# A two-layer diffusion trunk on one core: low parts of the weights by an accumulating DMA

## Chip, core and metric

The kernel runs on one core of a Trainium2 chip. The metric is the device time of one execution in microseconds. An engine keeps its own queue and works it in order; the queues wait for each other through semaphores. In the profile PE is TensorE (PEld its weight loads), DVE is VectorE, ACT is ScalarE, POOL is GpSimd, and SP is SyncE, which issues the DMAs of the kernel before.

## What is computed

Two layers over 256 latent tokens and 256 context tokens of width 1024 (the context is dropped after the second layer's mixer). Each layer is a half-step SwiGLU, a mixer (retention in layer 0, neighbourhood attention in layer 1) and another half-step SwiGLU, each behind an RMS norm with scale, shift and gate from a conditioning vector.

```python
def swiglu(x, w_in, w_out):
    a, b = jnp.split(x @ w_in, 2, axis=-1)
    return (jax.nn.silu(a) * b) @ w_out

for i in range(DEPTH):
    ml = (s_c @ w_mod[i] + b_mod[i]).reshape(-1, 3, 3, D)
    h = gated_residual(h, ml, 0, swiglu(ada_in(h, norm_g[i, 0], ml, 0), ffn_w_in[i, 0], ffn_w_out[i, 0]), 0.5)
    ...
    h = gated_residual(h, ml, 1, yl, 1.0)
    ...
    h = gated_residual(h, ml, 2, swiglu(ada_in(h, norm_g[i, 2], ml, 2), ffn_w_in[i, 1], ffn_w_out[i, 1]), 0.5)
return rms_norm(h, final_norm_g)
```

The hidden width is 2816; all inputs are float32.

## The kernel before

**Products in three parts.** The large products run in TensorE's float32r format. Each operand is split in a high part, rounded to that format, and a low part, the rest. A product is then three matmuls: high by high, high by low, low by high (`acc3`, line 623). So every weight tile gives two tiles, `whi` and `wlo`.

**The stream of weights.** `plan_all` lists 200 tiles in the order of use: 88 of `ffn_w_in` (1 MiB each, a tile is 128 partitions by 2048), 64 of `ffn_w_out` (128 by 1408, 704 KB), 32 of retention and 16 of neighbourhood attention (1 MiB each). `load` (272) takes the next one into one of two `raw` buffers by a DMA on SyncE's queue. `prep` (280) takes one of three `whi` and three `wlo` buffers and writes down, for each half of the tile, two steps: `first`, a copy on ScalarE from `raw` to `whi`, and `second`, a subtraction `raw - whi` to `wlo` on the engine in `state["low"]`. That is VectorE but for the first tile or two, whose first halves GpSimd makes (lines 1426 to 1454). `RAWS, SPLITS = 2, 3` (214) are the numbers of buffers. A tile's buffers come free when TensorE has used it up (`retire`, 333); `pump` (303) then splits and loads ahead.

**The order.** All engines but SyncE take their instructions in the order in which the program issues them. A small model of the engines' times (`account`, 131) sets that order while the program is built: after each matmul (`mm`, 261) `advance` (231) issues what is due, such as steps of `soon` (splits of weights), of `later` (normalisation, gating) and of the background. The background (`bg_steps`, 357) makes the conditioning's scale, shift and gate vectors on VectorE from 128 loads of 512 KB (`mraw`, `mod_load`, 348), a step every 2.2 us of the model; `mod_sum` (384) adds each result up in a `one` bank of PSUM while `state["sums"]` is set.

**Stages.** Feed-forward of layer 0, retention with four heads, feed-forward, feed-forward of layer 1, neighbourhood attention with 16 heads, and the last feed-forward, which serves the latent tokens alone. A feed-forward (`ffn`, 734) has two halves of 11 `win` tiles and 8 `wout` tiles. A `win` tile takes 48 matmuls, a `wout` tile 33; they are 512 columns wide for both streams, 258 or 256 in the last one. In each half the first two `wout` tiles run together: both products over ten of eleven parts, then the last part of each, and only then do the two tiles retire. In neighbourhood attention `weigh` (1233) subtracts a mask and a bias on GpSimd for each of 32 units before VectorE reads the scores.

Everything an engine computes through the wrapper `Engine` has line 151, a matmul line 262, a load of `dma` line 166.

Of the kernel before, what the change touches and what calls it, by code (L numbers as in the profile page):

```python
# [9 lines left out]
F32 = mybir.dt.float32  # L10
F32R = mybir.dt.float32r
I32 = mybir.dt.int32
AF = mybir.ActivationFunctionType
ALU = mybir.AluOpType
# [3 lines left out]
P = 128  # L18
# [53 lines left out]
def trunk(ctx, tc, a):  # L72
    nc = tc.nc
# [11 lines left out]
    def nm(s):  # L85
        uid[0] += 1
        return f"{s}_{uid[0]}"
# [8 lines left out]
    def slots2(shape, dt=F32R):  # L96
        return slot(shape, dt), slot(shape, dt)
# [17 lines left out]
    def pair():  # L115
        return ps_pair.tile([P, 2, 512], F32, tag="pair", name=nm("pair"))

    def one():
        return ps_one.tile([P, 512], F32, tag="one", name=nm("one"))
# [4 lines left out]
    now = {"pe": 0.0, "dve": 0.0, "act": 0.0, "pool": 0.0, "dma": 0.0}  # L124
    ready = {}
    HOP = 0.2

    def key(ap):
        return ap.tensor.name

    def account(e, reads, writes, us):
        start = now[e]
        for ap in reads:
            t, by = ready.get(key(ap), (0.0, e))
            start = max(start, t + (HOP if by != e else 0.0))
        now[e] = start + us
        for ap in writes:
            ready[key(ap)] = (now[e], e)
# [23 lines left out]
    A_ = Engine("act", nc.scalar, 0.09, 1200.0)  # L162
# [52 lines left out]
    raws, split_tiles = [], []  # L215
    state = {"loaded": 0, "freed": 0, "split": 0, "retired": 0, "bg_at": 0.0, "hold": True, "sums": True, "inside": True, "lag": (0.0, 0.0), "tight": False}
# [5 lines left out]
    soon = []  # L222
# [49 lines left out]
    def load():  # L272
        src = plan[state["loaded"]]
        state["loaded"] += 1
        w = src.shape[1] * src.shape[2]
        t = wpool.tile([P, 2048], F32, tag="raw", name=nm("raw"), bufs=RAWS)
        dma(out=t[:, :w], in_=src.rearrange("p x y -> p (x y)"))
        raws.append((t, src.shape))

    def prep():  # L280
        raw, shape = raws.pop(0)
        tile_no = state["split"]
        state["split"] += 1
        w = shape[1] * shape[2]
        hi = wpool.tile([P, 2048], F32R, tag="whi", name=nm("whi"), bufs=SPLITS)
        lo = wpool.tile([P, 2048], F32R, tag="wlo", name=nm("wlo"), bufs=SPLITS)
        m = w // 2
        for i, c in enumerate((slice(0, m), slice(m, w))):
            def first(c=c):
                A_.copy(out=hi[:, c], in_=raw[:, c])  # L290

            def second(c=c, i=i):
                state["low"].tensor_tensor(out=lo[:, c], in0=raw[:, c], in1=hi[:, c].bitcast(F32), op=ALU.subtract)
                if i == 1:
                    state["freed"] += 1
                    pump()

            soon.append((now["pe"] + state["lag"][0] + 0.3 + i, tile_no, first, 0, i, raw))
            soon.append((now["pe"] + state["lag"][1] + 1.5 + 1.2 * i, tile_no, second, 1, i, hi))
        soon.sort(key=lambda x: (x[1], x[3], x[4]))  # L300
        split_tiles.append((hi, lo, shape, tile_no))

# [30 lines left out]
    def retire(lag=(0.0, 0.0)):  # L333

        state["retired"] += 1
        state["lag"] = lag
        pump()
        state["lag"] = (0.0, 0.0)
# [125 lines left out]
    sums = {}  # L464
# [441 lines left out]
    def retention(xt, g, done, tab, m, lg):  # L906
# [37 lines left out]
        def proj_v(first):  # L944
            v = [slots2([P, 2, 512]) for _ in range(2)]
            if first:
                ps = [one() for _ in range(4)]
            else:
                pp = [pair(), pair()]
                ps = [pp[t // 2][:, t % 2, :] for t in range(4)]  # L950
            for kh in range(2):
                wh, wl = weight()
                for t in range(4):
                    o = ps[t]
                    for k in range(4):
                        xh = xt[2 * kh + k // 2][0][:, k % 2, t * P:(t + 1) * P]
                        xl = xt[2 * kh + k // 2][1][:, k % 2, t * P:(t + 1) * P]
                        mm(o, lhsT=xh, rhs=wh[:, k, :], start=kh == 0 and k == 0, stop=False)
                        mm(o, lhsT=xh, rhs=wl[:, k, :], start=False, stop=False)
                        mm(o, lhsT=xl, rhs=wh[:, k, :], start=False, stop=kh == 1 and k == 3)  # L960
                    if kh == 1 and first:
                        split(v[t // 2][0][:, t % 2, :], v[t // 2][1][:, t % 2, :], o)
                    elif kh == 1 and t % 2 == 1:
                        split(*v[t // 2], pp[t // 2])
                retire()
            return v

        def scores(q, k, m):
# [108 lines left out]
        for hd in range(H_RET):  # L1077
# [14 lines left out]
            if hd + 1 < H_RET:  # L1092
                m = masks(hd + 1, lg)
# [304 lines left out]
    rows, diag, scale = {}, {}, {}  # L1398
# [88 lines left out]
    for l in range(2):  # L1487
# [8 lines left out]
        else:  # L1496
            raw = neighbourhood(xt, GateLater(lambda: gate(1, 1, (L,), 1.0)), *mixer)
# [10 lines left out]
    y = rstd_rows(L)  # L1508
    for i in range(2):
        for t in range(2):  # L1510
            o, src = slot([P, 512]), out_ps[t][:, i, :]
# [65 lines left out]
```

## Time and profile before

| | us |
|---|---|
| median of 3 runs | 1953.93 (1952.76 to 1954.39) |
| the profiled execution's own time | 1954.45 |
| its span, from the first to the last instruction | 1952.6 |
| TensorE busy | 1923.6 (99%) |
| VectorE busy | 1355.9 (69%) |
| ScalarE busy | 687.2 (35%) |
| GpSimd busy | 89.5 (5%) |

The span is what the trace covers; 1.85 us of the execution lie outside it. Busy time leaves out waiting, branching and the issuing of DMAs. An engine that is busy for 99% of the span sets the time unless its work can be made shorter; the others matter where it waits for them. Matmuls overlap in the records, so the rate of TensorE is read from the number of matmuls in a stretch, not from the mean duration of one.

### The profile page before, as it was taken

What the parts mean: (1) busy time and instruction counts of PE and PEld (TensorE: products, weight loads), DVE (VectorE), ACT (ScalarE), POOL (GpSimd) and SP (SyncE); (2) the same over time, 40 slices, a digit from 0 to 9 for tenths busy, and PEclk for the clock granted to TensorE, in tenths of its full rate; (3) what the DMA queues carried; (4) which work ended last, traced back from release to release, by engine and by line L of the source; (5) the groups of instructions that cost most, each with busy time, mean ns of one, the idle gap of its engine ahead of it and who ended that gap; (6) DMA issues with size and microseconds to landing.
All of it is one profiled execution on the core that took longest, in us unless ns stands there. A gap on an engine that the chain in (4) does not pass through costs nothing.

```text
span 1952.6 us, 26160 instructions
## 1 busy us (share of the span) xinstructions
PE 1923.6 (99%) x10458; PEld 1661.6 (85%) x10458; DVE 1355.9 (69%) x2396; ACT 687.2 (35%) x1033; POOL 89.5 (5%) x116
## 2 busy tenths in 40 slices
PE   7999999999999999999999999999999999999998
PEld 3888888898888888898888889888888899989998
DVE  5676666678888888877667676767632588887665
ACT  4432232333323232342222223322222366665443
POOL 5000000010000000100000001000000101100000
PEclk7999999999999999999999999999999999999999
DMA  7333533434343433234353443555423345544553
GB/s 287 138 136 116 203 130 131 161 119 152 126 144 133 159 130 132 95 130 138 126 189 129 139 138 102 187 194 201 162 101 81 110 119 112 98 116 166 193 174 116
DMA packets 70090, 278.85 MB, mean 143 GB/s; under 512 B 23632, under 2 KB 23888, under 8 KB 52304
## 3 DMA queue, kind: packets, MB, share of 16 engines
q1 hardware_dynamic: 69968, 277.18, 43.3%
q8 instruction: 82, 1.34, 0.3%
q14 instruction: 40, 0.33, 0.1%
HBM read 276.11 MB, written 1.05 MB: 142 GB/s over the span
## 4 chain that ended last, share of the span: by engine, by line
PE 93%; DVE 3%; ACT 2%; DMA 1%; issue 1%; SPq 0%; DVEq 0%; ACTq 0%
PE pair L262 60%; PE one L262 32%; DVE slot L151 1%; DVE t L151 1%; PE one L268 1%; ACT slot L151 1%; ACT whi L151 1%; DVE wlo L151 1%; DVE few L151 0%; DMA h<-in_x 0%; ACT t L151 0%; DMA raw<-in_nv 0%; SPq L166 0%; DVE h L151 0%; DVE scl L151 0%
## 5 line engine op out<-in xcount | busy, mean ns | idle before, releaser
L262 PE MATMUL pair<-slot,whi 128*128 128x512 f32 (+2 forms) x4000 | 1037.8, 351 | 8.2 <-ACT slot L151 5.4
L262 PEld LDWEIGHTS pair<-slot,whi 128*128 128x128 f32 x4000 | 696.3, 190 | 105.6 <-ACT slot L151 6.0
L262 PE MATMUL pair<-slot,wlo 128*128 128x512 f32 (+2 forms) x2000 | 681.0, 349 | 0.0
L262 PE MATMUL one<-slot,whi 128*128 128x512 f32 (+1 forms) x1860 | 481.5, 347 | 0.0
L151 DVE TENSOR_TENSOR wlo<-raw,whi 128x1024 fp32r<-128x1024 f32 (+1 forms) x398 | 433.7, 1121 | 33.6 <-ACT whi L151 32.8
L151 ACT CAST whi<-raw 128x1024 fp32r<-128x1024 f32 (+1 forms) x400 | 365.0, 960 | 224.5 <-PE one L262 140.4
L262 PEld LDWEIGHTS pair<-slot,wlo 128*128 128x128 f32 x2000 | 371.7, 190 | 48.0
L262 PEld LDWEIGHTS one<-slot,whi 128*128 128x128 f32 x1860 | 325.9, 189 | 43.5
L262 PE MATMUL one<-slot,wlo 128*128 128x512 f32 (+1 forms) x930 | 323.1, 347 | 0.0
L151 DVE SCALAR_TENSOR_TENSOR acc<-mraw,sT,acc 128x512 f32<-128x512 f32 x392 | 278.9, 749 | 16.8 <-DMA mraw<-in_wmod 15.5
L151 ACT ACTIVATE t<-pair 128x512 f32<-128x512 f32 x66 | 39.5, 598 | 440.7 <-PE pair L262 440.7
L262 PEld LDWEIGHTS one<-slot,wlo 128*128 128x128 f32 x930 | 176.1, 189 | 21.6
L151 DVE TENSOR_TENSOR t<-pair,t 128x512 f32<-128x512 f32 x66 | 45.6, 691 | 201.8 <-ACT t L151 201.7
L151 DVE TENSOR_TENSOR slot<-t,slot 128x512 fp32r<-128x512 f32 (+2 forms) x144 | 88.2, 613 | 64.9 <-ACT slot L151 63.4
L151 DVE SCALAR_TENSOR_TENSOR h<-one,gate,h 128x256 f32<-128x256 f32 x112 | 49.6, 479 | 106.9 <-PE one L262 106.7
L151 ACT CAST slot<-t 128x512 fp32r<-128x512 f32 (+2 forms) x144 | 79.4, 551 | 123.0 <-DVE t L151 122.7
L151 POOL TENSOR_TENSOR t<-t,t 128x256 f32<-128x256 f32 (+1 forms) x48 | 40.6, 856 | 1687.3 <-ACT t L151 1265.8
L262 PE MATMUL pair<-whi,slot 128*128 128x512 f32 (+1 forms) x384 | 98.5, 339 | 0.0
L262 PE MATMUL one<-slot,slot 128*128 128x512 f32 (+1 forms) x432 | 89.8, 347 | 1.3 <-DVE slot L151 1.0
L151 ACT ACTIVATE t<-h 128x256 f32<-128x256 f32 (+1 forms) x86 | 35.8, 429 | 145.0 <-DVE h L151 129.9
L262 PEld LDWEIGHTS one<-slot,slot 128*128 128x128 f32 x432 | 69.9, 189 | 10.8 <-DVE slot L151 1.4
L262 PEld LDWEIGHTS pair<-whi,slot 128*128 128x128 f32 x384 | 67.1, 189 | 7.5
(103 smaller groups left out, 1103.3 us busy)
## 6 DMA issues: line engine op xcount, KB each, us to landing
raw<-in_win SPq DMA_DIRECT2D x88, 1024.0 KB, 4.9
mraw<-in_wmod SPq DMA_DIRECT2D x128, 512.0 KB, 4.6
raw<-in_wout SPq DMA_DIRECT2D x64, 704.0 KB, 4.1
slot<-in_wmod SPq DMA_DIRECT2D x16, 512.0 KB, 9.7
raw<-in_rv SPq DMA_DIRECT2D x8, 1024.0 KB, 4.8
raw<-in_rg SPq DMA_DIRECT2D x8, 1024.0 KB, 4.8
raw<-in_ro SPq DMA_DIRECT2D x8, 1024.0 KB, 4.9
slot<-in_ex SPq DMA_DIRECT2D x8, 512.0 KB, 5.5
```

The source lines that it names most:

```text
L151: getattr(self.real, op)(*args, **kw)
L262: nc.tensor.matmul(out, lhsT=lhsT, rhs=rhs, start=start, stop=stop)
L268: nc.tensor.transpose(out=out, in_=in_, identity=ident)
```

## The change

`second` no longer subtracts. ScalarE writes the negative of the high part to `wlo`, and a DMA on GpSimd's queue reads the same half tile of the weights from HBM once more and adds it to what stands there: `-whi + raw`. The model counts that DMA, half a tile each, and sets the low part as ready 3 us after it. `second` is due by the first lag, 0.9 us after `first`, instead of the second one. `raws` keeps the source's address for it. `raw` is read by ScalarE's copy alone. In the first head of retention `proj_v` holds `mod_sum` off while it uses its four `one` banks. The choice in `state["low"]` no longer matters.

```diff
-        raws.append((t, src.shape))
+        raws.append((t, src.shape, src))
 
     def prep():
-        raw, shape = raws.pop(0)
+        raw, shape, src = raws.pop(0)
...
             def second(c=c, i=i):
-                state["low"].tensor_tensor(out=lo[:, c], in0=raw[:, c], in1=hi[:, c].bitcast(F32), op=ALU.subtract)
+                A_.activation(out=lo[:, c], in_=hi[:, c].bitcast(F32), func=AF.Copy, scale=-1.0)
+
+                nc.gpsimd.dma_start(out=lo[:, c], in_=src.rearrange("p x y -> p (x y)")[:, c].bitcast(F32R), accum_op=ALU.add)
+                now["dma"] = max(now["dma"], now["act"])
+                account("dma", [], [lo], P * m * 4 / 340e3)
+                ready[key(lo)] = (now["dma"] + 3.0, "dma")
                 if i == 1:
                     state["freed"] += 1
                     pump()
 
             soon.append((now["pe"] + state["lag"][0] + 0.3 + i, tile_no, first, 0, i, raw))
-            soon.append((now["pe"] + state["lag"][1] + 1.5 + 1.2 * i, tile_no, second, 1, i, hi))
+            soon.append((now["pe"] + state["lag"][0] + 1.2 + i, tile_no, second, 1, i, hi))
...
             if first:
+
+                state["sums"] = False
                 ps = [one() for _ in range(4)]
...
+            state["sums"] = True
             return v
```

The order of the instructions at three places follows; a name's number is the tile's own, and x2 stands for two halves in a row.

ScalarE at the start, before (`whi_258` and `whi_260` are the first two weight tiles, `slot_262` and `slot_264` the first normalised chunks that TensorE multiplies):

```order
L151 CAST whi_258<-raw_113 128x1024
L151 ACTIVATE slot_262<-t_62_274,modT 128x256
L151 ACTIVATE slot_262<-t_63_277,modT 128x256
L151 ACTIVATE slot_264<-t_64_281,modT 128x256
L151 CAST whi_260<-raw_115 128x1024
L151 ACTIVATE slot_264<-t_65_287,modT 128x256
```

The same place of the change:

```order
L151 CAST whi_258<-raw_113 128x1024
L151 ACTIVATE wlo_259<-whi_258 128x1024
L151 ACTIVATE slot_262<-t_62_275,modT 128x256
L151 ACTIVATE slot_262<-t_63_278,modT 128x256
L151 ACTIVATE slot_264<-t_64_282,modT 128x256
L151 CAST whi_260<-raw_115 128x1024
L151 ACTIVATE wlo_261<-whi_260 128x1024
L151 ACTIVATE slot_264<-t_65_289,modT 128x256
```

One negation stands ahead of the first chunk and one ahead of the fourth.

ScalarE in the `win` tiles of the last feed-forward, before (`t` is the SiLU of a tile's product, `slot` the high part of the gated product):

```order
L151 CAST whi_15808<-raw_15741 128x1024 x2
L151 ACTIVATE t_2213_15879<-t_2212_15878,few_15881 128x256
L151 CAST slot_15877<-t_2214_15880 128x256
L151 CAST whi_15875<-raw_15832 128x1024 x2
L151 ACTIVATE t_2222_15947<-t_2221_15946,few_15949 128x256
L151 CAST slot_15945<-t_2223_15948 128x256
```

And of the change:

```order
L151 CAST whi_15977<-raw_15895 128x1024 x2
L151 ACTIVATE wlo_15978<-whi_15977 128x1024 x2
L151 ACTIVATE t_2187_16051<-t_2186_16050,few_16053 128x256
L151 CAST slot_16049<-t_2188_16052 128x256
L151 CAST whi_16047<-raw_15965 128x1024 x2
L151 ACTIVATE wlo_16048<-whi_16047 128x1024 x2
L151 ACTIVATE t_2196_16121<-t_2195_16120,few_16123 128x256
L151 CAST slot_16119<-t_2197_16122 128x256
```

Two negations come between the casts of a tile and the next SiLU.

GpSimd in neighbourhood attention, before (each row is the mask's subtraction for one or two units; `t` is the bias that a DMA brought):

```order
L151 TENSOR_TENSOR slot_11650<-slot_11650,t_1751_12745 128x256 x2
L151 TENSOR_TENSOR slot_11650<-slot_11650,t_1767_12861 128x256 x2
L151 TENSOR_TENSOR slot_11650<-slot_11650,t_1786_12985 128x256 x2
L151 TENSOR_TENSOR slot_11650<-slot_11650,t_1809_13092 128x256 x2
L151 TENSOR_TENSOR slot_11650<-slot_11650,t_1830_13195 128x256 x2
```

And of the change:

```order
L151 TENSOR_TENSOR slot_11932<-slot_11932,t_1751_13051 128x256 x2
L295 DMA wlo_13208<-in_nv 128x1024 x2
L151 TENSOR_TENSOR slot_11932<-slot_11932,t_1767_13169 128x256 x2
L295 DMA wlo_13327<-in_nq 128x1024 x2
L151 TENSOR_TENSOR slot_11932<-slot_11932,t_1786_13295 128x256 x2
L151 TENSOR_TENSOR slot_11932<-slot_11932,t_1810_13414 128x256
L295 DMA wlo_13474<-in_nk 128x1024 x2
L151 TENSOR_TENSOR slot_11932<-slot_11932,t_1810_13414 128x256
```

The accumulating DMAs stand between the subtractions in the same queue, two to a weight tile.

## Rows read from the trace of the kernel before

**Rows 1.** The page: its span and its first part, busy time by engine.
```profile
span 1952.6 us, 26160 instructions
PE 1923.6 (99%) x10458; PEld 1661.6 (85%) x10458; DVE 1355.9 (69%) x2396; ACT 687.2 (35%) x1033; POOL 89.5 (5%) x116
```
**Rows 2.** The page: the chain that ended last, by engine.
```profile
PE 93%; DVE 3%; ACT 2%; DMA 1%; issue 1%; SPq 0%; DVEq 0%; ACTq 0%
```
**Rows 3.** Waits of TensorE: who for whom, us in total, times, longest us.
```profile
PEld one L262 <- issue: 15.8, 26, 5.0
PEld pair L262 <- ACT slot L151: 6.0, 3, 3.5
PEld one L262 <- DVE t L151: 4.0, 3, 2.3
...
PEld pair L262 <- DVE t L151: 0.4, 2, 0.2
```
**Rows 4.** Windows: stretch, length, busy us (instructions) by engine, granted clock, DMA share, GB/s.
```profile
15.00:45.00 30.00, 22.33 (x99) 16.01 (x97) 24.50 (x39) 12.99 (x18) 21.71 (x19) 0.72 0.78 313
...
500.00:600.00 100.00, 100.00 (x459) 83.24 (x458) 82.98 (x147) 29.21 (x37) 0.00 (x0) 1.00 0.41 143
...
1300.00:1400.00 100.00, 100.00 (x447) 82.85 (x446) 68.78 (x116) 21.52 (x28) 0.00 (x0) 1.00 0.59 200
...
1800.00:1900.00 100.00, 100.00 (x832) 100.00 (x832) 64.27 (x98) 45.19 (x65) 0.00 (x0) 1.00 0.55 184
```
**Rows 5.** Groups by form, VectorE: busy us, mean ns, idle before, releaser.
```profile
L151 DVE TENSOR_TENSOR wlo<-raw,whi 128x1024 fp32r<-128x1024 f32 x270 | 321.7, 1221 | 19.2 <-ACT whi L151 18.7
...
L151 DVE TENSOR_TENSOR wlo<-raw,whi 128x704 fp32r<-128x704 f32 x128 | 112.0, 910 | 14.4 <-ACT whi L151 14.1
```
**Rows 6.** Groups by form, ScalarE.
```profile
L151 ACT CAST whi<-raw 128x704 fp32r<-128x704 f32 x128 | 93.0, 778 | 106.8 <-PE one L262 38.2 <-DMA raw<-in_wout 34.4 <-issue 32.7
...
L151 ACT ACTIVATE slot<-pair 128x1024 f32<-128x1024 f32 x4 | 4.1, 1029 | 24.3 <-PE pair L262 24.3
```
**Rows 7.** DMA queues (packets, MB, share) and issues (count, KB, us to landing).
```profile
q1 hardware_dynamic: 69968, 277.18, 43.3%
...
raw<-in_wout SPq DMA_DIRECT2D x64, 704.0 KB, 4.1
...
out_y<-slot SPq DMA_DIRECT2D x4, 256.0 KB, 2.4
```
**Rows 8.** DMA from 1800 to 1890 us: rate in 40 slices of 2.25 us.
```profile
GB/s 98 109 215 13 303 16 230 330 80 210 110 198 213 238 23 353 335 113 306 153 302 142 244 226 178 295 36 324 106 106 411 262 160 0 69 382 15 58 368 47
```
**Rows 9.** Timeline of SyncE's queue, last feed-forward: start, us, instruction.
```profile
1720.92 75.89 SPq L166 DMA_DIRECT2D raw<-in_win  x11
1802.55 30.03 SPq L166 DMA_DIRECT2D raw<-in_wout  x8
```
**Rows 10.** The tile raw: durations of one issue on SyncE (min/median/max ns).
```profile
L166 SPq DMA_DIRECT2D raw<-in_win x88: 327/328/430, 11.1 to 1889.6; - x88
```
**Rows 11.** Groups by form, GpSimd.
```profile
L151 POOL TENSOR_TENSOR slot<-slot,t 128x256 f32<-128x256 f32 x32 | 25.0, 782 | 144.9 <-DVE few L151 116.8 <-DMA t<-in_rpb 25.1 <-DVE slot L151 3.0
...
L151 POOL TENSOR_TENSOR wlo<-raw,whi 128x1024 fp32r<-128x1024 f32 x2 | 4.7, 2350 | 3.9 <-ACT whi L151 3.9
```
**Rows 12.** Timeline of TensorE at the start: start, us, instruction, idle before.
```profile
29.65 3.45 PE L262 MATMUL pair<-slot,whi 128*128 128x256 f32 x13 [3.39 <-ACT slot L151]
...
35.57 1.91 PE L262 MATMUL pair<-slot,wlo 128*128 128x256 f32 x8
```
**Rows 13.** Waits of SyncE's queue.
```profile
SPq L166 <- DVE wlo L151: 1327.8, 198, 28.0
```

## Prediction

> **What bounds the kernel now.** I read the page's busy line first: TensorE is busy 1923.6 of 1952.6 us, 99% of the span, so only 29 us can be won without taking matmuls away, and this change takes none away [rows 1]. The chain that ended last says the same: 93% of it is TensorE, 3% VectorE, 1% DMA [rows 2]. TensorE's own waits come next: its longest are start-up and hand-over waits of a few us each, and no row shows it waiting for `wlo` or `whi`; the splits are always ready in time [rows 3]. Then the stages: at 500 to 600 us 16 DMA engines are 41% busy, at 1300 to 1400 us 59%, and at 1800 to 1900 us 55% at 184 GB/s [rows 4]. That last stretch is the last feed-forward (22 `win` tiles, 16 `wout` tiles, latent tokens alone): 832 matmuls in 100 us, 0.120 us each, against 447 and 459, about 0.22 us each, in the full-width stretches of the same rows. There a weight tile is used up in half the time, and DMA has the least room.
>
> **What the change removes.** VectorE loses 398 subtractions, 321.7 + 112.0 = 434 us of its 1355.9 [rows 1, 5]. None of it is on the chain; VectorE is 69% busy and TensorE's waits on it (12 rows, under 4.1 us each, the largest in [rows 3]) come at hand-overs, where small dependent steps follow each other. I book 3 us of gain for shorter queues there.
>
> **What it adds on ScalarE.** 400 negations of half a tile. ScalarE's 128x1024 activation takes 1.03 us, its 704-wide cast 0.78 [rows 6]: 272 x 1.03 + 128 x 0.78 = 380 us on top of 687.2, 55% in all. In the last feed-forward it is 45% busy; two more ops of 1.03 us per 5.77 us (48 matmuls x 0.120) make 81%. It stays off the path, but every small copy that TensorE waits for may now stand behind a negation. I book 3 us, which cancels the gain above.
>
> **What it adds on DMA.** 400 accumulating transfers, a second reading of all weights: 88 x 1024 + 64 x 704 + 48 x 1024 KB = 180 MiB. The trace has no such transfer. What 16 engines need for a plain MiB, called u, has two rows: 43.3% of the span for 277.18 MB is 845 us for 264.3 MiB, 3.20 us [rows 7]; the best slice of the last feed-forward, 411 GB/s, gives 2.55 us [rows 8]. I take the middle, 2.87 us, since packets that wait for each other count as busy in the first and the second is a burst. An accumulate per MiB is at least one load (1 u). It is at most a load, a read of SBUF and a write, each priced like a whole transfer (3 u). I take 2 u: two streams are read, one from HBM like `raw`, one from SBUF like `out_y`, and one is written [rows 7]. With the first load a MiB of weights then costs 3 u = 8.6 us instead of 2.87. No run here prices an accumulate; the Trainium skill (Collectives: The Full Stack, Part 3, on the bandwidth ceiling) has a reducing transfer at half a copy's rate because both sources go through one read ring, and the sum by that price is the same as mine.
>
> *Last feed-forward.* It holds 22 x 1 + 16 x 0.6875 = 33 MiB and 22 x 48 + 16 x 33 = 1584 matmuls, 190.4 us at 0.120. Its loads go out from 1720.9 us on [rows 9]. Three tiles can be split ahead (SPLITS = 3), so 30 MiB must pass while it runs: 30 x 8.61 = 258 us. **258 - 190 = 68 us longer.** This is the main term.
>
> *Full-width stages.* A `win` tile has 48 x 0.224 = 10.8 us. It needs 8.6 us, and the background loads of modulation weights about half a MiB, 1.4 us: 10.0 us, hidden, but only just. Where those loads are densest, 1300 to 1400 us, 200 GB/s is 19.1 MiB, and 9.2 MiB of weights twice more: 37.5 MiB x 2.87 = 108 us in 100 [rows 4]. **8 us.**
>
> *Latency.* With three buffers a tile's low part has two tiles' time to appear, 21.6 us in `win`, which hides everything. Shortest is the place where two `wout` tiles run together and both retire at the end: one tile's time, 33 x 0.224 = 7.4 us. The chain there is two casts and a negation, 3 x 0.78 = 2.3 us [rows 6]; the issue on GpSimd, between SyncE's 0.33 us per DMA [rows 10] and the 2.35 us that GpSimd needs for a subtraction [rows 11], say 1.3; half a `wout` tile at 2 u, 2.0 us; and what landing takes beyond the bytes, 4.1 - 0.69 x 2.87 = 2.1 us [rows 7]. That is 7.7 us alone and some 8.8 beside another load: 1.4 us late at six such places. **8 us.** (The two in the last feed-forward are in its own term.)
>
> *Start.* GpSimd makes the first two low parts in 2.35 us each [rows 11]. TensorE waits 3.39 us for ScalarE's first normalised chunk at 29.65 us and takes the first `wlo` at 35.57 us [rows 12]; one negation now stands before that chunk, one more before its fourth. The accumulate leaves at about 28 us and needs 1.3 + 2.9 + 2.1 = 6.3 us, more beside a queue that is 78% busy from 15 to 45 us [rows 4]. Bounds 0 to 8 us; I take **4 us**.
>
> GpSimd's queue: each accumulate waits in order for its negation, and in neighbourhood attention 32 mask subtractions of 0.78 us stand behind such waits, with VectorE's score pass waiting for them [rows 11]. A negation is at most a few us late and two units of work lie between; I book nothing, and if that cover is gone it is about 1 us at each of 16 tiles. SyncE's queue gains: it waited 1327.8 us in all for VectorE's `wlo` before it could reload `raw`; now the cast alone frees it [rows 13]. That brings loads forward by up to two ScalarE ops and wins nothing, as no row of TensorE waits for them.
>
> **Sum.** 68 + 8 + 8 + 4 = 88 us on the profiled execution's own 1954.45 us (1.85 us of it outside the span), 2042.5; that execution is 0.5 us above the median, so **2042 us**.
>
> **The rivals.** *Hidden.* If the second queue's transfers cost 1 u, the last feed-forward needs 2 x 2.87 = 5.74 us per MiB against 190.4 / 33 = 5.77, and only half the latency and the start remain: about 1960 us, from 1950 to 1995. For it: no stage is above 59% busy now, so a second plain load would fit everywhere on average. Against: two streams must be read for one written. The trace has one data queue [rows 7] and cannot tell whether another has engines of its own; if it had, 2 u = 5.74 us would run beside 2.87 and the result be the same 1960. The Trainium skill (DMA: Bandwidth & Descriptors, "Issuing engines are not separate DMA queues") denies that: all queues share the 16 engines. No run here shows it yet; by it this half of the rival falls and the 88 us stand.
>
> *Dear.* At 3 u the last feed-forward needs 30 x 11.5 - 190 = 154 us more and all transfers together (264.3 + 3 x 180) x 2.87 = 2308 us, so DMA bounds the whole kernel: up to 2330 us; with u = 2.55 the same is 30 x 10.2 - 190 = 116 us and some 2090. Issue on GpSimd leads there too: 76 issues in 190 us leave 2.5 us each, and at 4 us each they cost 304 - 190 = 114 us. For it: GpSimd takes 2.35 us where VectorE takes 1.22 for the same subtraction [rows 5, 11], so slow issue is possible. A mechanism that would stretch the issue is VectorE holding GpSimd off SBUF while it works, 1356 - 434 = 922 us in all; an op of it is 922 us / (2396 - 398) = 0.46 us [rows 1, 5], and if each issue waited for one it would be 1.3 + 0.5 = 1.8 us, still under 2.5, so this alone gives 2042 and not more. The Trainium skill (SBUF — State Buffer, the box on the "DVE blocks DMA" trap) states such a lock for descriptors that GpSimd writes; no row shows it here.
>
> *Faster.* VectorE's relief outweighs the rest. TensorE's waits on VectorE sum to about 20 us over its rows, the largest 4.0 [rows 3]; half of them gone and accumulates free is 1954 - 8 = 1946 us. It decides if an accumulate costs 1 u or less and its landing under 7.4 us. Against it: those waits follow chains of small ops, not the subtractions.
>
> **How the numbers follow.** Forecast case (2000 to 2110 us) 0.48; hidden 0.22, of which 0.05 within 0.2%; dear 0.24; faster 0.06. A measurement of this kernel tells 0.2%, 3.9 us, from no change. So faster 0.06, same 0.05, slower 0.89. The range goes from 1958, above the faster and the unchanged cases (0.11 left out), to 2230, which leaves out the upper part of the dear case (0.09).
>
> **What would show it.** Right: DMA busy share at 0.9 and more in the last feed-forward and TensorE idle there, waiting for DMA into `wlo`, with some 68 us; nearly none in the full-width `win` stages; an accumulate of 512 KB that lands in 5 to 9 us. Wrong: a last feed-forward as long as before (hidden), waits for `wlo` in every stage (dear), GpSimd's issues back to back with idle DMA engines (issue bound), or waits of TensorE that name ScalarE.

## The result and the profile after

The changed kernel takes 2150.03 us (median of 4 runs, 2149.3 to 2150.5) against 1953.95 beside it: 1.100 times the time before, 95% interval 1.099 to 1.102. The forecast was 2042. The sign was right; the loss is 196 us where 88 were worked out.

The page of the kernel after, its span, busy times, DMA queues, chain, GpSimd's issues (busy us, mean ns) and landings (us), against [rows 1], [rows 2] and [rows 7]:

```profile
span 2147.5 us, 26873 instructions
PE 1987.4 (93%) x10458; PEld 1701.2 (79%) x10458; DVE 938.5 (44%) x1998; ACT 1032.7 (48%) x1433; POOL 428.7 (20%) x514
...
q0 software_dynamic: 57600, 188.77, 47.4%
q1 hardware_dynamic: 69968, 277.18, 38.3%
...
PE 70%; DMA 17%; ACT 6%; DVE 3%; issue 2%; POOL 1%; SPq 0%; ACTq 0%; DVEq 0%; POOLq 0%
...
L295 POOL DMA_DIRECT2D wlo<-in_win x176 | 153.2, 874 | 744.4 <-ACT wlo L151 733.2
...
L295 POOL DMA_DIRECT2D wlo<-in_wout x128 | 113.1, 981 | 360.0 <-ACT wlo L151 342.5
...
raw<-in_wout SPq DMA_DIRECT2D x64, 704.0 KB, 6.0
wlo<-in_wout POOLq DMA_DIRECT2D x128, 352.0 KB, 9.2
```

The 195 us of span split in two on the first two rows. TensorE's idle time went from 29.0 to 2147.5 - 1987.4 = 160.1 us, **131 more**. Its busy time grew by 1987.4 - 1923.6 = **64 us** for the same 10458 matmuls, so those took longer. The chain names DMA for 17% of the span, where it was 1%.

What TensorE waits for (who for whom, us in total, times, longest us), against [rows 3]:

```profile
PE pair L262 <- DMA wlo<-in_win: 67.0, 30, 7.4
PE one L262 <- DMA wlo<-in_wout: 35.6, 22, 4.6
PE one L262 <- DMA wlo<-in_rv: 9.5, 2, 8.3
PE pair L262 <- DMA wlo<-in_nk: 7.8, 3, 4.8
...
PE one L262 <- DVE slot L151: 4.4, 3, 2.0
```

Every large row is an accumulate into `wlo` that has not landed. Windows of the same trace, in the columns of [rows 4]:

```profile
15.00:45.00 30.00, 23.05 (x95) 16.12 (x96) 17.99 (x43) 16.54 (x23) 18.45 (x22) 0.66 0.96 350
...
100.00:200.00 100.00, 99.54 (x441) 82.06 (x440) 45.74 (x86) 41.60 (x55) 16.24 (x19) 1.00 0.89 227
500.00:600.00 100.00, 99.76 (x457) 82.71 (x456) 67.01 (x139) 48.06 (x56) 13.88 (x16) 1.00 0.84 229
1300.00:1400.00 100.00, 91.09 (x385) 74.36 (x384) 34.35 (x62) 38.67 (x48) 15.12 (x18) 0.93 0.92 250
...
1900.00:2000.00 100.00, 80.42 (x611) 78.03 (x610) 17.60 (x42) 57.03 (x78) 26.20 (x30) 0.95 1.03 254
```

Inside the full-width stages (100 to 200 us in the first feed-forward, 500 to 600 in retention) TensorE is busy for 99.5% and more, with DMA at 0.89 and 0.84: the accumulates are hidden there. From 1300 to 1400 us its 8.9 us of idle time are two waits of 4.5 and 4.4. In the last feed-forward (here 1867 to 2138 us) DMA is at 1.03 and the matmuls fall from 832 to 611 in 100 us. That stage as a whole, from its first matmul to its last, in the kernel before and after:

```profile
1748.80:1942.90 194.10, 193.41 (x1606) 193.04 (x1606) 127.02 (x209) 86.11 (x134) 5.86 (x7) 1.00 0.47 158
...
1867.40:2137.80 270.40, 216.30 (x1606) 208.46 (x1606) 54.67 (x137) 146.54 (x206) 68.19 (x79) 0.93 0.96 236
```

So where are the other losses? I took the time from the first matmul on a stage's first weight tile to that of the next stage (in the last one, to its last matmul), and subtracted the same time of the kernel before (us longer; FF is a feed-forward; "before last" sums the stages ahead of the last feed-forward). Counted from 0, the stages begin with the weight tiles 0, 38, 70, 108, 146 and 162. The column "us" is the median time, the others are from the profiled execution:

| kernel | us | FF 1 | retention | FF 2 | FF 3 | attention | before last | last FF |
|---|---|---|---|---|---|---|---|---|
| after | 2150.0 | 18.4 | 24.0 | 24.2 | 27.9 | 24.6 | 119 | 76 |
| e1_plain | 2056.4 | 6.9 | 14.3 | 15.8 | 17.2 | 16.6 | 71 | 32 |
| e2_neg_add | 2020.3 | 2.1 | 9.2 | 0.2 | 3.4 | 15.3 | 30 | 37 |
| e3_full_only | 2068.2 | 16.5 | 26.6 | 23.7 | 25.9 | 21.3 | 114 | 0 |
| e4_last_only | 2034.9 | 0.0 | 0.0 | 0.0 | 0.0 | 2.8 | 3 | 74 |
| e5_low_last | 2132.6 | 11.4 | 30.3 | 12.8 | 12.9 | 22.4 | 90 | 90 |
| e6_half | 2043.4 | 12.8 | 18.9 | 8.6 | 12.3 | 6.8 | 59 | 32 |
| e7_neg_first | 2153.0 | 18.9 | 23.3 | 19.1 | 29.0 | 31.0 | 121 | 77 |
| e9_early | 2161.7 | 20.5 | 29.1 | 29.6 | 31.1 | 23.1 | 133 | 76 |
| e10_thin | 2122.8 | 18.7 | 20.8 | 17.8 | 16.7 | 22.3 | 96 | 76 |
| e11_early_thin | 2128.8 | 18.0 | 23.5 | 19.7 | 18.4 | 24.0 | 104 | 73 |
| e12_no_gate | 2117.1 | 17.8 | 15.2 | 13.3 | 14.6 | 24.7 | 86 | 75 |
| e13_no_gate_thin | 2111.3 | 16.3 | 19.4 | 15.7 | 9.9 | 19.9 | 81 | 74 |
| e14_no_gate_low_full | 2016.0 | 9.9 | 10.0 | 12.1 | 8.4 | 21.6 | 62 | 1 |
| e15_raw_behind | 2133.0 | 13.5 | 17.1 | 18.0 | 17.5 | 31.3 | 98 | 81 |
| e16_raw_behind_no_gate | 2114.6 | 12.4 | 13.3 | 16.9 | 9.0 | 22.3 | 74 | 83 |

The last feed-forward lost 76 us, close to the 68 forecast. The stages ahead of it lost 119 where 20 had been booked (8 for full width, 8 for latency, 4 for the start). They lose most of it where one stage hands over to the next: of TensorE's 77 us of waits for low parts there, 43 stand at eight tiles right behind the start of a stage (39, 41, 71, 73, 109, 111, 147 and 148), 16 at the six places where two `wout` tiles run together, 7 at the start and 12 at other tiles. One such place in full: the feed-forward after retention, whose first two `win` tiles run together. The low part of the second, tile 71, lands too late. ScalarE, SyncE, GpSimd and TensorE there (start, us, instruction, idle before):

```profile
874.10 0.51 ACT L151 ACTIVATE slot<-t,modT 128x256 fp32r<-128x256 f32 x1 [0.88 <-DVE t L151]
874.88 0.51 ACT L151 ACTIVATE slot<-t,modT 128x256 fp32r<-128x256 f32 x1 [0.28 <-DVE t L151]
875.30 1.98 ACT L151 CAST whi<-raw 128x1024 fp32r<-128x1024 f32 x2
877.18 2.00 ACT L151 ACTIVATE wlo<-whi 128x1024 fp32r<-128x1024 f32 x2
...
877.30 0.33 SPq L166 DMA_DIRECT2D raw<-in_win  x1
...
878.54 1.81 POOL L295 DMA_DIRECT2D wlo<-in_win  x2 [6.52 <-ACT wlo L151]
...
886.18 2.07 PE L262 MATMUL pair<-slot,wlo 128*128 128x256 f32 x8 [4.59 <-DMA wlo<-in_win]
```

The buffer came free at about 865, with the last matmul on the tile that held it. ScalarE takes the two casts at 875.30, behind the normalisation's chunks; the negations follow, the accumulate of the first half leaves at 878.54, and its sum is there when TensorE goes on at 886.18: 21 us after the buffer was freed, 4.6 of them waited for. At the eight tiles the casts begin 4 to 10 us after the buffer is free, the first accumulate leaves 3 to 4 us later and lands 7 to 12 us after that, 17 to 25 us in all. In the kernel before, the first use of the low part came 12 to 16 us after the buffer was free. The DMA engines between 862 and 900 us, in 40 slices of 0.95 us (busy tenths, GB/s):

```profile
DMA  0000000000000000099999999989699699999200
GB/s 9 0 17 0 0 0 0 0 0 0 0 0 0 0 0 0 0 147 379 414 267 185 112 134 185 211 177 168 233 440 341 78 121 177 203 207 203 52 0 0
```

They are idle for 15 us and then full. The reload of `raw`, freed by the same casts, goes first at about 400 GB/s; the accumulates follow at 110 to 210. After the wait the clock is low (two windows):

```profile
884.60:891.40 6.80, 4.85 (x21) 4.56 (x22) 1.16 (x3) 4.23 (x6) 1.73 (x2) 0.50 0.99 246
...
895.30:902.10 6.80, 6.80 (x59) 6.80 (x58) 0.29 (x1) 0.60 (x1) 0.00 (x0) 1.00 0.33 66
```

At a granted clock of 0.50, 1.2 GHz, 21 matmuls take 4.85 us, 0.23 us each; at 1.00 (2.4 GHz) 59 take 6.80, 0.115. The trace has 22 such stretches, 159 us in all, against 4 before, 28 us; one goes with each of TensorE's 17 longest waits for a low part. TensorE is busy for 113 us of them, before for 18; at half the clock that makes (113 - 18) / 2 = 48 of the 64 us of busy time. The other 16 I did not trace. The mean granted clock fell from 0.993 to 0.963.

### The profile page after: what moved, and what is told of

The parts are those of the page before. It is cut to its first block, busy times and chain, and to the rows that moved or that the text cites. A ratio compares the mean times of both kernels' runs of the same rounds, so it can differ in the third digit from the quotient of the medians.

```text
span 2147.5 us, 26873 instructions
## 1 busy us (share of the span) xinstructions
PE 1987.4 (93%) x10458; PEld 1701.2 (79%) x10458; DVE 938.5 (44%) x1998; ACT 1032.7 (48%) x1433; POOL 428.7 (20%) x514
## 3 DMA queue, kind: packets, MB, share of 16 engines
q0 software_dynamic: 57600, 188.77, 47.4%
q1 hardware_dynamic: 69968, 277.18, 38.3%
## 4 chain that ended last, share of the span: by engine, by line
PE 70%; DMA 17%; ACT 6%; DVE 3%; issue 2%; POOL 1%; SPq 0%; ACTq 0%; DVEq 0%; POOLq 0%
PE pair L262 46%; PE one L262 23%; DMA wlo<-in_win 7%; DMA wlo<-in_wout 5%; ACT whi L151 2%; DMA wlo<-in_ro 2%; DVE t L151 2%; ACT wlo L151 2%; DVE slot L151 1%; ACT t L151 1%; POOL wlo L295 1%; ACT slot L151 1%; PE one L268 1%; DMA wlo<-in_nv 1%; DMA wlo<-in_rv 1%
## 5 line engine op out<-in xcount | busy, mean ns | idle before, releaser
L262 PE MATMUL pair<-slot,whi 128*128 128x512 f32 (+2 forms) x4000 | 1054.7, 355 | 4.2 <-ACT slot L151 3.0
L262 PEld LDWEIGHTS pair<-slot,whi 128*128 128x128 f32 x4000 | 710.8, 194 | 102.8 <-ACT slot L151 3.9
L262 PE MATMUL pair<-slot,wlo 128*128 128x512 f32 (+2 forms) x2000 | 702.3, 361 | 79.3 <-DMA wlo<-in_win 67.0
L262 PEld LDWEIGHTS pair<-slot,wlo 128*128 128x128 f32 x2000 | 385.9, 198 | 137.2 <-DMA wlo<-in_win 74.7
L262 PE MATMUL one<-slot,whi 128*128 128x512 f32 (+1 forms) x1860 | 489.1, 352 | 0.0
L151 ACT ACTIVATE wlo<-whi 128x1024 fp32r<-128x1024 f32 (+1 forms) x400 | 366.8, 965 | 0.3
L262 PEld LDWEIGHTS one<-slot,whi 128*128 128x128 f32 x1860 | 331.8, 193 | 44.2
L262 PE MATMUL one<-slot,wlo 128*128 128x512 f32 (+1 forms) x930 | 330.6, 355 | 38.3 <-DMA wlo<-in_wout 35.6
L295 POOL DMA_DIRECT2D wlo<-in_win x176 | 153.2, 874 | 744.4 <-ACT wlo L151 733.2
L295 POOL DMA_DIRECT2D wlo<-in_wout x128 | 113.1, 981 | 360.0 <-ACT wlo L151 342.5
## 6 DMA issues: line engine op xcount, KB each, us to landing
wlo<-in_win POOLq DMA_DIRECT2D x176, 512.0 KB, 10.3
```

The costliest lines, as they stand in the source:

```text
L151: getattr(self.real, op)(*args, **kw)
L262: nc.tensor.matmul(out, lhsT=lhsT, rhs=rhs, start=start, stop=stop)
L295: nc.gpsimd.dma_start(out=lo[:, c], in_=src.rearrange("p x y -> p (x y)")[:, c].bitcast(F32R), accum_op=ALU.add)
```

## The experiments

In the diffs a minus is the kernel after, but for e8.

**e3 and e4: which stages.** The accumulate where the condition holds, VectorE's subtraction with its old due time elsewhere (e4: `tile_no >= 160`). The last feed-forward has 38 tiles, 162 to 199, and not the 40 of the two expectations: tiles 160 and 161 are the last two of attention. Where expectations speak of 121 and 75 us, the table has 119 and 76.

```diff
-                A_.activation(out=lo[:, c], in_=hi[:, c].bitcast(F32), func=AF.Copy, scale=-1.0)
+                if tile_no < 160:
+                    A_.activation(out=lo[:, c], in_=hi[:, c].bitcast(F32), func=AF.Copy, scale=-1.0)
...
+                else:
+                    state["low"].tensor_tensor(out=lo[:, c], in0=raw[:, c], in1=hi[:, c].bitcast(F32), op=ALU.subtract)
```

> Accumulates for weight tiles 0 to 159, the subtraction on VectorE as before for the last feed-forward's 40 tiles. Theory that the stages' losses add: the last feed-forward's 75 us go, 2150 - 75 = 2075 us, within 10. If the loss in the full-width stages were only what was forecast (20 us): 1975 us.

> The subtraction on VectorE as before for weight tiles 0 to 159, accumulates for the last feed-forward's 40 tiles. Theory that the last feed-forward is bound by the DMA engines at 3 copies' time per MiB: 1954 + 75 = 2029 us, within 10. If its loss came from work left over from the crowded stages before it: under 2000 us.

Measured 2068.2 and 2034.9 us, both as expected. Their losses, 114 and 80 us, add up to the whole; the 3 us of e4 in attention are those two tiles. e4's last feed-forward is full as in the changed kernel (window 1830 to 1930):

```profile
1830.00:1930.00 100.00, 78.96 (x567) 75.47 (x567) 14.44 (x35) 54.82 (x73) 26.10 (x30) 0.92 1.03 257
```

So there are two separate losses: that of a stage that is short of DMA, and that of the stages ahead of it.

**e1: the second reading as a plain copy.** `wlo` then holds the weights themselves.

```diff
-                nc.gpsimd.dma_start(out=lo[:, c], in_=src.rearrange("p x y -> p (x y)")[:, c].bitcast(F32R), accum_op=ALU.add)
+                nc.gpsimd.dma_start(out=lo[:, c], in_=src.rearrange("p x y -> p (x y)")[:, c].bitcast(F32R))
```

> The changed kernel with the DMA on GpSimd's queue as a plain copy instead of an accumulate: wlo holds the weights themselves, so the low parts are not computed; the same 400 DMAs, bytes from HBM, negations and order. Price theory (an accumulated packet takes the engines twice as long, so accumulates land after 9 to 10 us where 11 to 16 us of lead less ScalarE's 3 to 4 us are there): packets of 4096 bytes fall from 327 to about 160 ns, landing falls to 5 to 7 us, TensorE's waits for wlo mostly go and the time is 1960 to 2000 us. Rival, the queue itself (issue and descriptors on GpSimd, or sharing the engines with SyncE's loads) makes them late: 2080 us or more.

2056.4 us, ratio 1.052 [1.049, 1.055], between the two. Its queues and GpSimd's group:

```profile
q1 hardware_dynamic: 69968, 277.18, 40.6%
q0 software_dynamic: 57600, 188.77, 28.1%
...
L295 POOL DMA_DIRECT2D wlo<-in_win x176 | 93.5, 531 | 757.2 <-ACT wlo L151 750.8
```

28.1% of 2052.9 us for 180 MiB is 3.20 us per MiB, and 47.4% of 2147.5 was 5.65: the accumulation itself costs 0.77 of a copy more. Without it 94 us are gained: 45 in the last feed-forward, 48 ahead of it. But 71 us stay ahead of it, and 26 of the 43 us of waits at the eight tiles, so the rate is not the whole of the hand-overs.

**e2: no second reading.** ScalarE's negation stays, VectorE adds `raw` to it.

```diff
-                nc.gpsimd.dma_start(out=lo[:, c], in_=src.rearrange("p x y -> p (x y)")[:, c].bitcast(F32R), accum_op=ALU.add)
-                now["dma"] = max(now["dma"], now["act"])
-                account("dma", [], [lo], P * m * 4 / 340e3)
-                ready[key(lo)] = (now["dma"] + 3.0, "dma")
+                V.tensor_tensor(out=lo[:, c], in0=raw[:, c], in1=lo[:, c].bitcast(F32), op=ALU.add)
```

> The changed kernel without its DMAs: ScalarE's negations stay in their places, VectorE adds the raw weights to them instead of the accumulating DMA. Theory that the DMA is the whole loss: 1954 to 1962 us, DMA share back to about 0.43, granted clock back to 0.99. Rival, the 367 us of negations in ScalarE's queue hold up the small copies that TensorE waits for: over 1990 us, with waits of TensorE that name ScalarE.

2020.3 us, 1.034 [1.031, 1.037]. Ahead of the last feed-forward 30 us are left, so some 89 of the 119 come with the DMA. In the last one 37 us appear that are this edit's own, as the first row of TensorE's waits says; the second row is VectorE's group of additions:

```profile
PE pair L262 <- DVE wlo L151: 24.2, 22, 2.3
...
L151 DVE TENSOR_TENSOR wlo<-raw,wlo 128x1024 fp32r<-128x1024 f32 x272 | 325.8, 1224 | 198.6 <-ACT wlo L151 198.1
```

For the last stage it is no test of a kernel without the DMA. Ahead of it VectorE stands still for negations too, and its other steps stand behind these additions in its queue; the waits of TensorE that name ScalarE sum to 8 us only. So the 30 us are not the price of ScalarE's work alone.

**e5 and e8: the low part last.** In each `win` and retention-v tile the matmuls with `wlo` stand behind all the others; e8 is the same edit to the kernel before.

```diff
-                for ab in range(2):
-                    acc3(ps[:, ab, wide], xterms(xt, wh, wl, slice(ab * P, ab * P + P), wide))
...
+                for out, terms_ in both:
+                    for i_, (h_, _, xh, xl) in enumerate(terms_):
+                        mm(out, lhsT=h_, rhs=xh, start=i_ == 0, stop=False)
+                        mm(out, lhsT=h_, rhs=xl, start=False, stop=False)
+                for out, terms_ in both:
+                    for i_, (_, l_, xh, xl) in enumerate(terms_):
+                        mm(out, lhsT=l_, rhs=xh, start=False, stop=i_ == KC - 1)
```

> The changed kernel, but TensorE runs a tile's matmuls with the low part of the weights after all those with the high part (both column halves of a win tile, each wout product, each half of retention's v), so wlo is wanted up to 7 us later in a full-width tile and 3.8 us later in the last feed-forward; the matmuls are the same. Lateness theory (in the full-width stages the engines keep up on average and the accumulates only land too late for the 11 to 16 us of lead after hand-overs): most of the 94 us of the full-width feed-forwards and retention go, the last feed-forward, bound by the engines' rate, stays at +60 to +75; in all 2040 to 2080 us. Rival, the rate of the engines bounds the full-width stages too: later use only moves the waits, 2110 us or more.

> Control: the kernel before with the same order of matmuls as the run with low parts last. Nothing there waits for wlo, so the order itself should cost nothing: 1950 to 1960 us.

e8 is at 1.000 [0.999, 1.001], so the order as such costs nothing. e5 took 2132.6 us, in the rival's stretch: the loss of the feed-forwards ahead of the last fell from 71 to 37 us, but that of retention rose by 6 and that of the last one by 13. A lateness of a few us that this order would cover is part of the loss, and not all of it.

**e6: half the accumulates** (condition `i == 1`, as in e3).

> Accumulates for the second half of every weight tile, VectorE's subtraction as before for the first half. DMA then needs 2 copies' time per MiB of weights instead of 3, and the accumulated half is wanted half a tile later. By the price of 2 copies per accumulate: last feed-forward 2 x 2.87 = 5.74 us per MiB against 5.77 us of matmuls, so it is near balance: +0 to +20 us there and under 20 us elsewhere, 1955 to 1995 us. If each accumulate is late whatever the load (latency of its own): over 2040 us.

2043.4 us, far from balance. The last feed-forward lost 32 us, 21 of them in eight waits for accumulates, yet half the bytes would have fitted: 30 x (3.11 + 2.83) = 178 us of DMA in a stage of 194 before. An accumulate still landed after 8.7 us (median of 512 KB), so it can be late where its bytes fit.

**e7: negation right behind its cast**, `soon` sorted by half before step.

> The changed kernel with the order of ScalarE's steps in a tile changed from cast, cast, negation, negation to cast, negation, cast, negation, so the first accumulate can leave one cast (1.0 us) sooner. If lateness is what costs: 1 us less at some 20 waits of the full-width stages and part of the half-clock stretches after them, 2115 to 2140 us. If only the engines' rate counts: no change, 2145 to 2155 us.

2153.0 us, no gain. At tile 71 the first accumulate leaves 2.4 instead of 3.2 us after the casts begin, but lands 9.9 instead of 7.6 us later: what ScalarE saves is lost in landing.

**e9 and e12: earlier in the order.** e9 sets the lags of `retire` to 0; e12 drops, besides, the old condition that holds split steps until the model's VectorE is free.

```diff
-        state["lag"] = lag
+        state["lag"] = (0.0, 0.0)
...
-        while soon and not state["tight"] and soon[0][0] <= now["pe"] and ready_at(soon[0][5]) <= now["pe"] + 0.3 and free("dve", 0.5):
+        while soon and not state["tight"] and soon[0][0] <= now["pe"] and ready_at(soon[0][5]) <= now["pe"] + 0.3:
```

> All lags of the retire calls set to 0, so at the hand-overs each cast and negation, and with it the accumulate, goes out up to 18 us earlier in the program's order; nothing else changes. Order theory (the waits at the hand-overs are accumulates that left too late, behind ScalarE's normalisation): the stages before the last feed-forward lose at most half of their 121 us, so 2080 to 2115 us. Rate theory (the accumulates stand behind other transfers): 2140 to 2155 us, as before the edit. Third case, ScalarE's normalisation is pushed back by the casts: over 2155 us.

> Lags 0 as before, and the split steps no longer wait in the program's order until the model's VectorE is free (a condition from the time when VectorE made the low parts). At the hand-over before tile 71 the casts of the changed kernel stand at 875.3 us, about 10 us after the buffer was freed at 865; without lags alone they stood in the same place. Order theory: hand-over waits of 4 to 5 us fall under 2 us, the stages before the last feed-forward lose at most half of their 121 us, 2080 to 2115 us. Rate theory: 2140 to 2165 us. Third case, ScalarE's early casts hold the normalised chunks back: waits of TensorE that name ACT slot, no gain.

e9 took 2161.7 us, and its trace shows why it was no test of the order: at the place above the casts still stand behind the same chunks (881.28, all of it 6 us later), and at tiles 39, 109 and 147 the first cast comes 8 us sooner but the negation stays 9 us behind it. It was not the lag that held them. The time lies in the third case's stretch, but the waits for ScalarE's chunks did not grow; those for low parts ahead of the last feed-forward did, from 77 to 88 us. e12 took 2117.1 us, 1.084 [1.078, 1.090], and lost 86 us ahead of the last feed-forward instead of 119 (its profiled execution is the faster of two that lie 9 us apart): the order theory's direction, but over a quarter of the loss and not the half it asked for. At the same hand-over the accumulate now leaves at 861.76, and TensorE waits for something else; the last three rows are its waits for normalised chunks in the whole run:

```profile
861.76 1.81 POOL L295 DMA_DIRECT2D wlo<-in_win  x2 [0.76 <-ACT wlo L151]
...
865.62 0.58 PE L262 MATMUL pair<-slot,whi 128*128 128x256 f32 x1 [3.91 <-DVE slot L151]
...
PE one L262 <- DVE slot L151: 10.1, 7, 3.4
PE pair L262 <- DVE slot L151: 8.9, 6, 3.9
PE pair L262 <- ACT slot L151: 5.5, 9, 1.9
```

The wait of 4.59 us for the low part is gone, and one of 3.91 for a normalised chunk has come. Over the eight tiles the casts now begin 1 to 4 us after the buffer is free, and the waits for low parts fall from 43 to 14 us; in the whole run those for chunks on VectorE and ScalarE rise from 11 to 26. So the order of the casts was a cause of the late low parts. ScalarE has two more us of work per tile at a place where the next stage's input passes through it; whichever goes first, the other is late. Before, the subtraction ran on VectorE and ScalarE had only the casts.

**e10, e11, e13: without the background loads.** `mod_load` reuses its first two tiles.

```diff
+            if len(loaded) > 1:
+                loaded.append(loaded[-2])
+                return
```

> 124 of the 128 background loads of modulation weights (62 MiB) are left out, and VectorE reads the first two again and again; the output is not the reference's for that reason. Rate theory: the full-width stages and neighbourhood attention lose at most half of their 121 us, so 2085 to 2110 us. Order theory: at most 15 us better, 2135 to 2150 us. Either way the last feed-forward, whose own loads fill it, keeps 60 us or more of its 75.

> Both edits at once: lags 0 and 124 background loads left out. If lateness at the hand-overs and crowding by other loads are all there is outside the last feed-forward, its 75 us alone remain: 2030 to 2050 us. If a third cause holds them (the time of an accumulate by itself, or ScalarE), over 2080 us.

> The same, and 124 of the 128 background loads of modulation weights left out (the output is not the reference's for that reason). If the order and the crowding by other loads are two separate causes, their gains add: the gain of the run without the condition, plus 27 us (what thinning gave alone). If thinning only shortens what comes out too late, it gives under 10 us here.

2122.8, 2128.8 and 2111.3 us. Alone, the edit gives 27 us, between the two theories' bounds; on top of e12 it gives 6 (the intervals overlap), as if it only shortened what comes out too late. The third cause that e11 asked for is there: 104 us stay ahead of the last feed-forward. At the eight tiles e10 leaves 41 of the 43 us. Crowding adds to the loss and is not what makes those accumulates late.

**e15 and e16: the reload behind the accumulates.** e16 has e12's edits too.

```diff
-    def dma(out, in_):
-        nc.sync.dma_start(out=out, in_=in_)
+    def dma(out, in_, q=nc.sync):
+        q.dma_start(out=out, in_=in_)
...
-        dma(out=t[:, :w], in_=src.rearrange("p x y -> p (x y)"))
+        dma(out=t[:, :w], in_=src.rearrange("p x y -> p (x y)"), q=nc.gpsimd if state["loaded"] > 5 else nc.sync)
```

> From the sixth weight tile on, the reload of raw is issued on GpSimd's queue, behind the accumulates of the tile whose casts freed it, instead of on SyncE's at the moment of the casts (877.3 us for the hand-over before tile 71, when the first accumulate leaves at 878.5). Collision theory: 1 MiB of plain load, about 3 us of all 16 engines, no longer runs ahead of the accumulates; each wait of 2 to 5 us before a low part shrinks by 1.5 to 3 us, median landing of an accumulate falls from 10 to about 8 us, and the stages before the last feed-forward lose 40 to 80 instead of 121 us: 2080 to 2115 us. Rate theory (the same bytes in another order): the waits move to whi and raw, 2140 us or more. In the last feed-forward both expect no gain or a loss.

> The same together with lags 0 and without the condition on VectorE. If the collision with the reload and the late order are separate causes, their gains add (35 us of order and those of the run before): 2050 to 2085 us; if they are one, no better than the better of the two alone.

e15 took 2133.0 us and lost 98 ahead of the last feed-forward. An accumulate lands 1.8 us earlier (10.3 before), the reload later (7.5 before):

```profile
wlo<-in_win POOLq DMA_DIRECT2D x176, 512.0 KB, 8.5
raw<-in_win POOLq DMA_DIRECT2D x83, 1024.0 KB, 11.3
```

At the eight tiles no cast waits for the later reload, and TensorE's waits fall from 43 to 33 us; elsewhere ScalarE's casts do wait for it, 248 us in all against 4. The collision is real and worth 22 us ahead of the last feed-forward, about half of the least that I expected. Together with the order (e16, 2114.6 us, far from 2050 to 2085) the time is no better than e12's within the spread of the two executions of each. Ahead of the last feed-forward 45 of the 119 come back, less than 33 + 22, so in part they shorten the same waits. In the last feed-forward both lose some us more, as expected.

**e14: the best accumulating version.** e12, e5's order, and VectorE's subtraction in the last feed-forward and the two tiles ahead of it.

> Without the condition and lags, with the low-part matmuls last in each win and retention-v tile, and VectorE's subtraction in the last feed-forward: the best accumulating version I can name. If order and lateness are what holds the stages before the last feed-forward, 1970 to 2010 us; if the accumulates' own rate does, over 2030 us.

2016.0 us, 1.032 [1.029, 1.035], between the bounds. TensorE's waits:

```profile
PE pair L262 <- DVE slot L151: 8.9, 6, 3.9
PE one L262 <- DMA wlo<-in_wout: 8.6, 6, 2.5
PE pair L262 <- DMA wlo<-in_win: 6.8, 3, 3.0
PE one L262 <- DVE slot L151: 6.2, 5, 3.5
PE pair L262 <- ACT slot L151: 5.5, 9, 1.5
```

Waits for accumulates fell from 103 us on the two large rows to 15 (the last feed-forward has none now), and those for normalised chunks lead. No version beats the kernel before.

## Why the prediction was right and wrong

- **TensorE bounds, 29 us to win.** Right; VectorE's relief, 1355.9 - 938.5 = 417 us, bought nothing. The 3 us of gain booked for it are not seen.
- **Price of an accumulate, 2 u with u = 2.87.** Right, with two small errors that cancel: 38.3% of 2147.5 us for 264.3 MiB is 3.11 us a MiB, more than 2.87; the accumulate, 5.65, is 1.8 times as much, less than 2, and so nearly the 5.74 forecast. The Trainium skill's half rate for a reducing transfer (Collectives: The Full Stack, Part 3) has 2 in that place; the measured 1.8 is a little better.
- **Last feed-forward, 68 us.** Right: 76. At the measured prices 30 MiB need 30 x (3.11 + 5.65) = 263 us, and the stage is 270 long, 194 before, with DMA at 0.96; e3 and e4 set it apart. Of the 76 us TensorE waits 52 for low parts and matmuls take 23 more. Not three tiles but two were ready at its start: the accumulate of the third, tile 164, left 14 us later and brings the longest wait of the stage, 7.4 us.
- **Full-width stages, 8 us, "hidden, but only just".** Right inside the stages, as the windows from 100 and 500 us show. Of the 8 us booked from 1300 to 1400 us one wait of 4.4 came, at tile 115; the other wait there, at tile 111, belongs to a hand-over.
- **Latency, 8 us: the step that failed.** It put the shortest cover at the paired `wout` tiles, and took "two tiles' time, 21.6 us" for every `win` tile. At the paired places TensorE waits 1.2 to 4.6 us, 16 in all, twice the forecast. But a stage's first tiles run in pairs too, and there the cover is 12 to 16 us (from the free buffer to the first use of the low part, in the kernel before). The chain priced at 7.7 to 8.8 us took 21 us in the place shown: 10 on ScalarE's order, which the sum did not have, 3 for casts and the first negation, 8 from the issue to the landing, behind the reload. Some 43 us are waited for at eight tiles of four such hand-overs, and e12 takes 29 of them away by an earlier place in ScalarE's order. An accumulate of 512 KB landed after 10.3 us (median), above the 5 to 9 given as a sign.
- **A term that was not there: the clock.** 64 us more of busy time, some 48 of them at 0.50 after waits. Of the 64 some 41 lie ahead of the last feed-forward (119 less the 78 by which TensorE's idle time grew there), where the sum had nothing for them.
- **ScalarE, 3 us that "cancels".** It was busy 345 us more (380 forecast), and wrong in kind: e12's waits for chunks, 15 us more, and the casts that come late at hand-overs name the place. e2, with the negations and no second DMA, loses 30 us ahead of the last feed-forward, though not by ScalarE alone.
- **SyncE's queue, "wins nothing".** It costs: the reload freed earlier runs ahead of the accumulate, 22 us by e15.
- **Start, 4 us.** The first feed-forward's first half lost 10.6 us, with waits of 2.9 and 3.4 us for the two halves of its first low part.
- **GpSimd's queue in neighbourhood attention, nothing.** The stage lost 25 us, 18 of them gone with half of the accumulates (e6) and 9 with none (e2). That its mask subtractions stand behind accumulates was not tried alone.
- **The rivals.** Hidden fell: both queues together take 86% of 16 engines and reach 1.03 in a window, and `raw<-in_wout` lands after 6.0 us, 4.1 before [rows 7]. That is one set of engines, as the Trainium skill has it (DMA: Bandwidth & Descriptors, "Issuing engines are not separate DMA queues"). Dear fell too, though 2150 lies in its stretch: the price is near 2 u, and an issue takes 0.87 to 0.98 us, far from the 2.5 at which it would lead; its sign, waits for `wlo` in every stage, came from another cause.

It stays open how the last 62 us of e14 divide; 22 of them are in neighbourhood attention. The edits that helped shorten one chain at different links, so their gains cannot be added, and I name no single cause. A fourth pair of split buffers, which would lengthen the cover, was not tried.

## What to carry to other kernels

Price a transfer that takes over an engine's step twice: by its bytes where its stage is nearest full, and by its whole chain, from the free buffer to the landing with the order of the engine that feeds it, where the cover is shortest; that is at hand-overs, not in the steady loop. On a kernel whose TensorE is 99% busy count a wait of a few us with what follows it at half clock. When a step moves to another engine, look for conditions in the program's order, and for reloads, that were tied to the engine it left.

## What the runs showed of the hardware

- An accumulating DMA took 5.65 us of 16 engines per MiB, a plain copy from the same queue 3.20 (e1); behind the reload at the hand-over shown it ran at 110 to 210 GB/s, the plain load at about 400.
- Its issue took GpSimd 0.87 us for 128x1024, a plain one 0.53 (e1), SyncE's 0.33 [rows 10].
- TensorE's longest waits for low parts each went with a stretch at 0.50 of the clock; a third of this change's loss, 64 of 195 us, stands in TensorE's busy time and in no row of waits, and some 48 of the 64 are such stretches.
